# Other costs in the scheduler of a transformer trunk's kernel, and its mLSTM output gate as a product of pairs

## The chip, the cores and the metric

One core of a Trainium2 chip. The time is the device time of one execution in microseconds (us), the median of three runs. Engines: PE is TensorE (matrix products), DVE VectorE, ACT ScalarE, POOL GpSimd; SP issues most of the DMAs.

## The reference

Two decoder layers on 256 tokens of width 1024, all in float32: first an mLSTM layer, then a differential-attention layer with a shared K and V. Each layer adds four sub-layers to x, each between two RMS norms: a half-step FFN, the mixer, a second half-step FFN and a per-layer input embedding. What the change touches is the end of the mLSTM mixer:

```
proj = x @ w_in
q, k, v, o, gates = jnp.split(proj, ...)
...
h = mlstm_chunkwise(q, k, v, log_i, log_f)
h = rms_norm(h, head_norm[:, None, :])
...
return (jax.nn.sigmoid(o) * h) @ w_out
def swiglu(x, w_in, w_out):
    gate, up = jnp.split(x @ w_in, 2, axis=-1)
    return (jax.nn.silu(gate) * up) @ w_out
```

The output gate o is a 256 x 1024 by 1024 x 1024 product, as v is.

## The kernel before

The tokens are two tiles t of 128 rows. A float32 product is made of three fp32r products per 128-row slice of the contraction: high half by high half, low half of the weight by high half of x, high half of the weight by low half of x (`mm3`). Weights come as 1 MB tiles 128x2048 from HBM into eight raw buffers (`wraw`); ACT copies the high half (`whi`), DVE subtracts it for the low half (`wlo`), into six pairs of buffers. In the traces the bank of a product's sum is `accI` (three banks; products by input weights) or `accO` (by output weights, and the heads' numerators), `tr` is the bank of transposes.

`in_block` gives one tile's 512 columns of a product: 8 slices by 3 matmuls, 24. `block_pair` gives both tiles by 1024 columns at once as a 2x2 block product in the manner of Strassen and Winograd: seven products (`times`, 12 matmuls each) where eight would do it plainly. For that it needs sums of weight blocks: `t3` and `u1` are sums made by DMA (a plain load by SP, then an accumulating load on the same buffer by POOL), `wt2` and `wt4` sums made by DVE on top; sums of x blocks (`forms`: s1, s2, s3, n4), and sums of the products (DVE, with the first operand copied out of its bank by ACT, `held`). Before the change block_pair serves the pairs of FFN blocks and the mLSTM's v; the output gate is four `in_block`s (`gate(t, b)`), each followed by a sigmoid on ACT.

In the mixer `outputs(t)` turns the heads' numerators into `hns[t]`: it sums denominators on PE (the 128x1 matmuls), works on 128x4 tiles on DVE, takes a power on POOL (`mhalf`), normalises, and scales the numerators with four DVE operations. `gated(t, b)` multiplies a half of `hns[t]` by the sigmoid and transposes it for the output projection (`out_proj`). Then comes the norm after the sub-layer: squares on ACT, two operations 128x1 on POOL, scaling on DVE, and the transposes for the next sub-layer.

The order is not written out by hand. A first pass records all operations (`Notes`); `play` then simulates a list scheduler with a cost for each operation (`cost`: `dur` is how long it occupies its engine, `lat` when its result is there) and picks, engine by engine, what comes next, and which buffer a tile gets. A second pass issues the operations in that order (all from one line, L389, so the profile's groups tell them apart by tile). DMAs get a landing time from their size; accumulating ones are on a queue of their own. Each engine runs its own queue in order; buffers and data are guarded by semaphores.

## Time and profile before

| | |
|---|---|
| runs | 1012.2, 1009.74, 1011.77 us; median 1011.77 |
| profiled execution | 1012.75 us, of which the span of the trace is 1011.0 |
| busy in the span | PE 99%, weight loads 81%, DVE 84%, ACT 67%, POOL 8% |
| moved by DMA | 262.11 MB, 259 GB/s in the mean |
| granted clock, mean | 0.998 |

The profile's page begins with the busy time of each engine, then shows the span in 40 slices (each digit the busy share in tenths), the chain of work that ended last, and groups of instructions. In a timeline a row has start, length, engine, operation, output and inputs, shapes and count, and in brackets how long the engine was idle before it and what released it.

### The profile page before, as it was taken

To read this page: it belongs to the slowest core of one execution; us is meant where nothing else is said; L and a number is where in the kernel's file an instruction comes from. 1 tells how busy PE (TensorE), PEld (TensorE's weight loads), DVE (VectorE), ACT (ScalarE), POOL (GpSimd) and SP (SyncE) were. 2 spreads that over 40 slices of the span, in tenths; PEclk is the share of its full clock that TensorE was granted. 3 is DMA by queue.
4 is the path that set the end of the run, shared out by engine and by line. 5 is a ranking of instruction groups with operands and counts; after the bars stand their busy time and mean duration, and the time that the engine had idled before them with its cause. 6 is when DMAs were issued, how large, how long until landed. Compare 5 with 4: busy or idle time off the path is not lost.

```text
span 1011.0 us, 12465 instructions
## 1 busy us (share of the span) xinstructions
PE 996.6 (99%) x4692; PEld 815.2 (81%) x4692; DVE 847.1 (84%) x886; ACT 674.3 (67%) x909; POOL 77.3 (8%) x118
## 2 busy tenths in 40 slices
PE   9999999999999999999999999999999999999997
PEld 7887787888878888888887888778778888888786
DVE  6999895888879899987888898986985899999783
ACT  7666683667657767656875677766866767768372
POOL 0000000100121000001110000000101200000010
PEclk9999999999999999999999999999999999999999
DMA  9999974955699788765779998784556997897631
GB/s 341 395 308 296 306 279 152 279 206 198 247 318 277 251 290 263 282 257 172 292 259 327 321 300 301 240 322 170 201 217 235 311 263 235 293 303 269 229 124 43
DMA packets 44132, 262.11 MB, mean 259 GB/s; under 512 B 5288, under 2 KB 5672, under 8 KB 15912
## 3 DMA queue, kind: packets, MB, share of 16 engines
q1 hardware_dynamic: 39176, 227.50, 58.7%
q0 software_dynamic: 4608, 33.56, 17.1%
q8 instruction: 37, 0.61, 0.2%
q10 hardware_dynamic: 288, 0.27, 0.1%
q14 instruction: 23, 0.19, 0.1%
HBM read 250.82 MB, written 10.49 MB: 258 GB/s over the span
## 4 chain that ended last, share of the span: by engine, by line
PE 83%; DMA 7%; DVE 6%; issue 2%; ACT 1%; POOL 0%; SPq 0%; DVEq 0%; POOLq 0%; ACTq 0%
PE accI L389 51%; PE accO L389 28%; DMA wraw<-in_ffn_in 5%; PE tr L389 4%; DVE wraw L389 1%; DVE wlo_4r L389 1%; DMA wraw<-in_x 1%; DVE wlo_3r L389 1%; DMA wraw<-in_xT 1%; DMA att<-in_diff_lambda 1%; DVE wlo_2r L389 1%; DVE wlo_1r L389 1%; DVE att L389 1%; DVE wlo_5r L389 0%; DVE sm L389 0%
## 5 line engine op out<-in xcount | busy, mean ns | idle before, releaser
L389 ACT ACTIVATE whi_0r<-wraw 128x2048 fp32r<-128x2048 f32 (+2 forms) x51 | 74.9, 1477 | 17.1 <-PE accI L389 4.9
L389 ACT ACTIVATE whi_1r<-wraw 128x2048 fp32r<-128x2048 f32 (+2 forms) x52 | 74.7, 1449 | 9.5 <-DMA wraw<-in_ffn_in 3.8
L389 ACT ACTIVATE whi_5r<-wraw 128x2048 fp32r<-128x2048 f32 (+1 forms) x49 | 72.6, 1493 | 9.5 <-DMA wraw<-in_ffn_in 2.5
L389 ACT ACTIVATE whi_2r<-wraw 128x2048 fp32r<-128x2048 f32 (+1 forms) x45 | 70.2, 1571 | 9.3 <-DMA wraw<-in_ffn_in 5.8
L389 ACT ACTIVATE whi_3r<-wraw 128x2048 fp32r<-128x2048 f32 (+1 forms) x47 | 72.2, 1546 | 5.4 <-PE accI L389 2.6
L389 ACT ACTIVATE whi_4r<-wraw 128x2048 fp32r<-128x2048 f32 (+1 forms) x44 | 69.8, 1599 | 8.5 <-DMA wraw<-in_ffn_in 3.4
L389 DVE TENSOR_TENSOR wraw<-wraw,wraw 128x2048 f32<-128x2048 f32 x32 | 73.0, 2282 | 0.1
L389 ACT ACTIVATE att<-accI 128x512 f32<-128x512 f32 x64 | 38.1, 596 | 27.1 <-PE accI L389 26.7
L389 POOL DMA_DIRECT2D wraw<-in_ffn_in x30 | 26.8, 893 | 370.6 <-DMA wraw<-in_ffn_in 287.2
L389 ACT ACTIVATE sg<-accI,sm 128x256 f32<-128x256 f32 x43 | 20.2, 470 | 41.4 <-PE accI L389 30.7
L389 DVE TENSOR_TENSOR wlo_4r<-wraw,whi_5r 128x2048 fp32r<-128x2048 f32 (+1 forms) x25 | 44.0, 1770 | 1.8 <-ACT whi_5r L389 1.8
L389 DVE TENSOR_TENSOR wlo_1r<-wraw,whi_0r 128x2048 fp32r<-128x2048 f32 (+1 forms) x25 | 43.9, 1771 | 1.5 <-ACT whi_0r L389 1.5
L389 DVE TENSOR_TENSOR wlo_5r<-wraw,whi_1r 128x2048 fp32r<-128x2048 f32 (+1 forms) x24 | 44.0, 1839 | 0.1
L389 POOL TENSOR_SCALAR sm<-sm 128x1 f32<-128x1 f32 x32 | 18.6, 582 | 327.3 <-ACT waste L389 327.2
L389 DVE TENSOR_TENSOR wlo_0r<-wraw,whi_0r 128x2048 fp32r<-128x2048 f32 (+2 forms) x24 | 41.8, 1751 | 2.0 <-ACT whi_0r L389 2.0
L389 DVE TENSOR_TENSOR wlo_2r<-wraw,whi_3r 128x2048 fp32r<-128x2048 f32 (+1 forms) x23 | 41.6, 1819 | 1.8 <-ACT whi_3r L389 1.8
L389 DVE TENSOR_TENSOR wlo_1r<-wraw,whi_1r 128x2048 fp32r<-128x2048 f32 (+2 forms) x26 | 42.0, 1626 | 1.1 <-ACT whi_1r L389 1.0
L389 DVE TENSOR_TENSOR wlo_3r<-wraw,whi_4r 128x2048 fp32r<-128x2048 f32 (+1 forms) x22 | 41.5, 1895 | 1.5 <-ACT whi_4r L389 1.5
L389 DVE TENSOR_TENSOR wlo_2r<-wraw,whi_2r 128x2048 fp32r<-128x2048 f32 (+1 forms) x22 | 41.5, 1896 | 1.0 <-ACT whi_2r L389 0.9
L389 DVE TENSOR_TENSOR wlo_4r<-wraw,whi_4r 128x2048 fp32r<-128x2048 f32 (+1 forms) x22 | 41.4, 1896 | 0.7 <-ACT whi_4r L389 0.7
L389 DVE TENSOR_TENSOR wlo_3r<-wraw,whi_3r 128x2048 fp32r<-128x2048 f32 (+1 forms) x22 | 41.5, 1895 | 0.4 <-ACT whi_3r L389 0.4
L389 DVE TENSOR_TENSOR wlo_0r<-wraw,whi_2r 128x2048 fp32r<-128x2048 f32 (+1 forms) x23 | 41.5, 1818 | 0.0
(488 smaller groups left out, 3033.7 us busy)
## 6 DMA issues: line engine op xcount, KB each, us to landing
wraw<-in_ffn_in SPq DMA_DIRECT2D x99, 1024.0 KB, 7.8
wraw<-in_ffn_out SPq DMA_DIRECT2D x44, 1024.0 KB, 10.2
wraw<-in_ffn_in POOLq DMA_DIRECT2D x30, 1024.0 KB, 11.8
wraw<-in_mlstm_in SPq DMA_DIRECT2D x13, 1024.0 KB, 4.8
wraw<-in_ple_gate SPq DMA_DIRECT2D x8, 1024.0 KB, 5.3
wraw<-in_w_kv SPq DMA_DIRECT2D x8, 1024.0 KB, 4.8
home<-wraw SPq DMA_DIRECT2D x28, 256.0 KB, 4.0
wraw<-home SPq DMA_DIRECT2D x14, 512.0 KB, 3.3
```

The lines of the kernel that those rows point to most:

```text
L389: getattr(getattr(self.nc, eng), name)(*args, **kw)
```

## The change

The change has five parts. The scheduler's costs: ACT and DVE operations occupy their engine 100 and 85 ns less, and their results come 100 and 85 ns after that (before 40 and 50); ACT sums and float32 matmuls cost otherwise; an operation that uses a result of its own engine, other than PE, waits for the result and not only for the engine. DMA: the bytes of plain and of accumulating transfers share the transfer engines one third to two thirds while both have some, and the landing times of all that are under way are worked out again with each new issue. In `block_pair` the load of b11 stands first and that of u1 behind b21. The output gate goes through `block_pair`, with `opened` called as each block is there. At the start, eight matmuls on zeros stand where twelve did.

```diff
@@ -214,27 +214,32 @@
         if o.name == "dma_start":
             size = math.prod(c for s, c in outs[0].ap) * 4
             o.dur = {"sync": 450, "scalar": 450, "gpsimd": 900}[o.eng]
-            o.lat = size / (165.0 if o.kw.get("accum_op") is not None else 400.0)
+            o.lat = size / (200.0 if o.kw.get("accum_op") is not None else 390.0)
         elif o.eng == "tensor":
             if o.name == "transpose":
                 o.dur, o.lat = 109, 310
             elif ins[0].dtype == F32R:
                 o.dur, o.lat = n / 2.4 + 14, n / 2.4 + 215
             else:
-                o.dur = max(n * 4 / 2.4 + 6, 70)
+
+                o.dur = max(n * 4 / 2.4 / (2 if ins[0].ap[0][1] == 64 else 1) + 6, 70 if n * 4 < P else 105)
+                if n == 1:
+                    o.dur = 210
                 o.lat = o.dur + 270
         elif o.eng == "scalar":
             ptr = any(k in o.kw and isinstance(o.kw[k], bass.AP) for k in ("scale", "bias"))
-            o.dur = 0.83 * m + (200 if sb_in else 172) + (90 if ptr else 0)
-            o.lat = o.dur + (110 if o.kw.get("accum_out") is not None else 0) + 40
+
+            sums = o.kw.get("accum_out") is not None
+            o.dur = 0.83 * m + (100 if sb_in else 72) + (90 if ptr else 0) + (90 if sums else 0)
+            o.lat = o.dur + (110 if sums else 0) + 140
             f = o.args[2] if len(o.args) > 2 else None
             o.table = f if f in (AF.Silu, AF.Exp, AF.Ln, AF.Sigmoid) else None
         elif o.eng == "vector":
             one = o.name in ("tensor_copy", "tensor_scalar", "memset") and len(sb_in) == len(ins)
-            o.dur = m / 0.96 / (2 if one else 1) + 155 + (60 if o.name == "scalar_tensor_tensor" else 0)
+            o.dur = m / 0.96 / (2 if one else 1) + 70 + (60 if o.name == "scalar_tensor_tensor" else 0)
             if o.name == "tensor_tensor_scan":
-                o.dur = 680
-            o.lat = o.dur + 50
+                o.dur = 600
+            o.lat = o.dur + 135
             o.two = len(sb_in) > 1
         elif o.eng == "gpsimd":
             o.dur = 560 if o.name == "tensor_tensor" else 320 + m
...
@@ -287,8 +294,35 @@
         for o in ops:
             if not o.left:
                 waiting[o.eng].append(o)
-        dma_free = add_free = 0.0
+
+        flow = {False: [], True: []}
+        flow_at = 0.0
         landed = []
+        freed = {}
+
+        def step(queues, t, until, done):
+            while t < until:
+                act = [k for k in queues if queues[k] and queues[k][0][0] <= t]
+                share = {k: 1.0 if len(act) == 1 else (1 / 3, 2 / 3)[k] for k in act}
+                stop = min([until] + [t + queues[k][0][1] / share[k] for k in act]
+                           + [q[0][0] for k, q in queues.items() if q and k not in act])
+                for k in act:
+                    queues[k][0][1] -= (stop - t) * share[k]
+                    if queues[k][0][1] < 1e-6:
+                        done(queues[k].pop(0)[2], stop)
+                t = stop
+                if not any(queues.values()):
+                    break
+
+        def later(q, t):
+            t += 400
+            if t > q.end:
+                q.end = t
+                for u in q.users:
+                    if u.start is None and u.after[q]:
+                        u.ready = max(u.ready, t)
+                for v in freed.get(q, ()):
+                    given[v] = max(given[v], t)
         lock_until = 0.0
         before = "r"
         table = AF.Silu
...
@@ -337,18 +371,15 @@
             waiting[e].remove(o)
             o.start = s
             if o.name == "dma_start":
-                if o.kw.get("accum_op") is None:
-                    begin = max(s + 1900, dma_free)
-                    dma_free = begin + o.lat
-                    o.end = dma_free + 400
-                    if e != "gpsimd":
-                        landed.append(o.end)
-                else:
-
-                    begin = max(s + 4000, add_free)
-                    add_free = begin + o.lat
-                    dma_free = max(dma_free, begin) + o.lat
-                    o.end = add_free + 4000
+                adds = o.kw.get("accum_op") is not None
+                o.end = s
+                if s > flow_at:
+                    step(flow, flow_at, s, lambda q, t: None)
+                    flow_at = s
+                flow[adds].append([s + (2600 if adds else 1700), o.lat, o])
+                step({k: [list(q) for q in v] for k, v in flow.items()}, flow_at, 1e12, later)
+                if e != "gpsimd":
+                    landed.append(o)
                 clock[e] = s + o.dur
             else:
                 end = s + o.dur
@@ -369,7 +400,7 @@
             for u in o.users:
                 u.left -= 1
                 if u.after[o]:
-                    u.ready = max(u.ready, o.end if u.eng != e or o.name == "dma_start" else clock[e])
+                    u.ready = max(u.ready, o.end if u.eng != "tensor" or e != u.eng else clock[e])
                     if u.eng != e:
                         u.far = max(u.far, o.end)
                 else:
...
@@ -503,7 +536,7 @@
     wz = T([P, P], "h", 2)
     nc.vector.memset(wz, 0.0)
     warm = trp()
-    for i in range(12):
+    for i in range(8):
         nc.tensor.matmul(warm[:, :P], wz, wz, start=True, stop=True)
 
 
@@ -673,12 +706,12 @@
             return parts(out)
 
         nc.is_urgent = False
+        b11 = load(src[0])
         t3 = load(src2[0], src2[1])
-        u1 = load(src[0], src2[0])
-        b11 = load(src[0])
         w11 = parts(b11)
         b21 = load(src[1])
         w21 = parts(b21)
+        u1 = load(src[0], src2[0])
         wt2 = add(b11, b11, t3)
         wu1 = parts(u1)
         wt3 = parts(t3)
@@ -1030,15 +1063,6 @@
             hns.append(hn)
 
 
-        wg_ = [in_weights(a["mlstm_in"][4 + b], m=2) for b in range(2)]
-        sos = {}
-
-        def gate(t, b):
-            pi = acc_in()
-            in_block(pi, xts[t], wg_[b])
-            sos[t, b] = piece()
-            nc.scalar.activation(sos[t, b], pi, AF.Sigmoid, scale=rs[t])
-
         uts = [None, None]
 
         def gated(t, b):
@@ -1048,15 +1072,23 @@
             nc.vector.tensor_tensor(hns[t][:, c], hns[t][:, c], sos[t, b], op=ALU.mult)
             to_xt4(hns[t], 4 * b, uts[t])
 
-        gate(0, 0)
-        outputs(0)
-        gated(0, 0)
-        gate(0, 1)
-        gated(0, 1)
-        outputs(1)
-        for b in range(2):
-            gate(1, b)
-            gated(1, b)
+        sos = {}
+
+        def opened(b, t, src):
+            sos[t, b] = piece()
+            nc.scalar.activation(sos[t, b], src, AF.Sigmoid, scale=rs[t])
+            if (t, b) == (0, 0):
+                outputs(0)
+                gated(0, 0)
+            elif (t, b) == (1, 1):
+                outputs(1)
+            elif (t, b) == (0, 1):
+                gated(0, 1)
+            else:
+                gated(1, 0)
+                gated(1, 1)
+
+        block_pair(xts, xf, a["mlstm_in"][4], a["mlstm_in"][5], opened)
         return out_proj(uts, a["mlstm_out"], gbc, epilogue)
```

How the order changes, at four places. The names are those of buffers and what went into them; a number behind a name is the buffer's.

DVE in the gate stretch, before: from the end of v's last split to `hns[0]`. `sm4` are the small tiles of `outputs(0)`; the four SCALAR_TENSOR_TENSOR write `hns[0]`; `att_4` in the last row is a sigmoid.

```order
L389 TENSOR_TENSOR wlo_4r_75<-wraw_3_80,whi_4r_69 128x2048
L389 TENSOR_TENSOR att_7_112<-accI_2_99,att_7_112 128x512
L389 TENSOR_TENSOR wlo_5r_76<-wraw_4_81,whi_5r_70 128x1024 x2
L389 TENSOR_TENSOR wlo_1r_72<-wraw_6_83,whi_1r_66 128x1024 x2
L389 TENSOR_TENSOR wlo_0r_71<-wraw_2_79,whi_0r_65 128x1024 x2
L389 TENSOR_TENSOR wlo_2r_73<-wraw_7_84,whi_2r_67 128x1024 x2
L389 TENSOR_TENSOR sm4_13_143<-sm4_12_142,sm4_11_141 128x4
L389 TENSOR_SCALAR sm4_14_144<-sm4_13_143 128x4
L389 TENSOR_TENSOR sm4_16_146<-sm4_10_140,sm4_15_145 128x4
L389 SCALAR_TENSOR_TENSOR wraw_3_80<-accO_2_102,sm4_16_146,wraw_0_77 128x256 x2
L389 SCALAR_TENSOR_TENSOR wraw_3_80<-accO_3_103,sm4_16_146,wraw_0_77 128x256 x2
L389 TENSOR_TENSOR wraw_3_80<-wraw_3_80,att_4_109 128x512
```

The same stretch in the new order, in two pieces. First the sums and splits at its head (`wlo_5` is b11, `wlo_1` b21, `wlo_3` t3, `accO` and `h` belong to the last heads):

```order
L422 TENSOR_TENSOR wlo_5r_76<-wraw_7_84,whi_5r_70 128x2048
L422 TENSOR_TENSOR att_7_112<-accI_2_99,att_7_112 128x512
L422 TENSOR_TENSOR wraw_7_84<-wraw_7_84,wraw_1_78 128x2048
L422 SCALAR_TENSOR_TENSOR att_4_109<-accO_3_103,at_0_127,h_1_114 128x256
L422 SCALAR_TENSOR_TENSOR att_4_109<-accO_3_103,at_0_127,h_1_114 128x128
L422 TENSOR_TENSOR wlo_1r_72<-wraw_3_80,whi_1r_66 128x2048
L422 SCALAR_TENSOR_TENSOR att_2_107<-accO_0_100,att_4_109 128x384
L422 TENSOR_TENSOR wlo_3r_74<-wraw_1_78,whi_3r_68 128x2048
```

And from the split of wt2 (`wlo_0`) through `hns[0]` to that of wt4 (`wlo_5`); `wraw_3` there is the sum wt4:

```order
L422 TENSOR_TENSOR wlo_0r_71<-wraw_7_84,whi_0r_65 128x2048
L422 TENSOR_TENSOR sm4_13_143<-sm4_12_142,sm4_11_141 128x4
L422 TENSOR_SCALAR sm4_14_144<-sm4_13_143 128x4
L422 TENSOR_TENSOR wraw_3_80<-wraw_3_80,wraw_7_84 128x2048
L422 TENSOR_TENSOR sm4_16_146<-sm4_10_140,sm4_15_145 128x4
L422 SCALAR_TENSOR_TENSOR wraw_1_78<-accO_2_102,sm4_16_146,wraw_0_77 128x256 x2
L422 SCALAR_TENSOR_TENSOR wraw_1_78<-accO_1_101,sm4_16_146,wraw_0_77 128x256 x2
L422 TENSOR_TENSOR wraw_1_78<-wraw_1_78,att_7_112 128x512
L422 TENSOR_TENSOR wlo_2r_73<-wraw_2_79,whi_2r_67 128x2048
L422 TENSOR_TENSOR xl_2r_95<-tr_0_104,xh_2r_91 128x512
L422 TENSOR_TENSOR wlo_4r_75<-wraw_6_83,whi_4r_69 128x2048
L422 TENSOR_TENSOR wlo_5r_76<-wraw_3_80,whi_5r_70 128x2048
```

An addition of 128x2048 stands ahead of b21's split, and another between the operation that POOL waits for and the one that waits for POOL; the four gate splits that were behind each other are now spread, and seven.

POOL at the end of the mLSTM mixer, before. `sm4_15` and `sm4_2` are the powers of `outputs`, the 128x1 pairs the norms after the projection:

```order
L389 TENSOR_TENSOR sm4_15_145<-sm4_14_144,mhalf_0_129 128x4
L389 TENSOR_TENSOR sm4_2_132<-sm4_1_131,mhalf_0_129 128x4
L389 DMA wraw_3_80<-in_ffn_in 128x2048
L389 DMA wraw_4_81<-in_ffn_in 128x2048
L389 TENSOR_SCALAR sm1_1_169<-sm4_4_134 128x1
L389 TENSOR_TENSOR sm1_3_171<-sm1_1_169,mhalf_0_129 128x1
L389 TENSOR_SCALAR sm1_2_170<-sm4_5_135 128x1
L389 TENSOR_TENSOR sm1_5_173<-sm1_2_170,mhalf_0_129 128x1
```

And in the new order:

```order
L422 DMA wraw_5_82<-in_mlstm_in 128x2048
L422 DMA wraw_1_78<-in_mlstm_in 128x2048
L422 DMA wraw_2_79<-in_mlstm_in 128x2048
L422 TENSOR_TENSOR sm4_15_145<-sm4_14_144,mhalf_0_129 128x4
L422 TENSOR_TENSOR sm4_2_132<-sm4_1_131,mhalf_0_129 128x4
L422 TENSOR_SCALAR sm1_1_169<-sm4_4_134 128x1
L422 TENSOR_TENSOR sm1_3_171<-sm1_1_169,mhalf_0_129 128x1
L422 TENSOR_SCALAR sm1_2_170<-sm4_5_135 128x1
L422 TENSOR_TENSOR sm1_5_173<-sm1_2_170,mhalf_0_129 128x1
L422 DMA wraw_3_80<-in_ffn_in 128x2048
```

The two accumulating loads of the next FFN's weights stood ahead of both norms; now the first stands behind them and the second further on. Three accumulating loads of the gate and v stand ahead of the powers.

DVE in the first FFN where PE waited for `hl_2` at 120.96 us, before:

```order
L389 SCALAR_TENSOR_TENSOR h_0_113<-att_0_105,sm1_4_172,sg_1_122 128x256
L389 TENSOR_TENSOR wlo_4r_75<-wraw_0_77,whi_4r_69 128x2048
L389 TENSOR_TENSOR wraw_0_77<-wraw_0_77,wraw_4_81 128x2048
L389 TENSOR_TENSOR hl_2r_120<-tr_0_104,hh_2r_117 128x256
L389 TENSOR_TENSOR wlo_5r_76<-wraw_6_83,whi_5r_70 128x2048
```

And in the new order:

```order
L422 SCALAR_TENSOR_TENSOR h_0_113<-att_0_105,sm1_4_172,sg_1_122 128x256
L422 TENSOR_TENSOR wlo_5r_76<-wraw_5_82,whi_5r_70 128x2048
L422 TENSOR_TENSOR wraw_4_81<-wraw_4_81,wraw_0_77 128x2048
L422 TENSOR_TENSOR hl_2r_120<-tr_0_104,hh_2r_117 128x256
L422 TENSOR_TENSOR wraw_5_82<-wraw_5_82,wraw_4_81 128x2048
```

The sum of weights (`wraw` from two `wraw`) still stands directly ahead of `hl_2`.

SP around the load of lambda (`in_diff_lambda`), near 662 us, before:

```order
L389 DMA wraw_3_80<-in_ffn_out 128x2048
L389 DMA wraw_2_79<-in_ffn_out 128x2048
L389 DMA att_7_112<-in_diff_lambda 128x256
L389 DMA wraw_6_83<-in_ffn_out 128x2048
L389 DMA wraw_5_82<-in_diff_q 128x2048
```

And in the new order:

```order
L422 DMA wraw_7_84<-in_ffn_out 128x2048
L422 DMA wraw_0_77<-in_diff_q 128x2048
L422 DMA wraw_3_80<-in_diff_q 128x2048
L422 DMA att_2_107<-in_diff_lambda 128x256
L422 DMA wraw_4_81<-in_diff_q 128x2048
```

It stood between loads of `ffn_out` and stands behind two of `diff_q`. Where DVE comes to it (the first 128x64 row), in the new order:

```order
L422 TENSOR_TENSOR wlo_2r_73<-wraw_3_80,whi_3r_68 128x1024
L422 TENSOR_TENSOR att_1_106<-att_1_106,att_2_107 128x512
L422 TENSOR_TENSOR wlo_2r_73<-wraw_3_80,whi_3r_68 128x1024
L422 SCALAR_TENSOR_TENSOR h_1_114<-att_1_106,sm1_1_169,sg_0_121 128x256
L422 TENSOR_TENSOR att_4_109<-accI_2_99,att_4_109 128x512
L422 TENSOR_TENSOR wlo_3r_74<-wraw_4_81,whi_4r_69 128x1024 x2
L422 TENSOR_TENSOR wlo_4r_75<-wraw_6_83,whi_5r_70 128x2048
L422 TENSOR_TENSOR att_1_106<-att_2_107 128x64
L422 TENSOR_TENSOR hl_2r_120<-tr_0_104,hh_2r_117 128x256
```

The second `diff_q` load goes to `wraw_3`, which the second row with `wlo_2` frees; four rows of DVE work lie between that and the 128x64 row.

8 lines of the change are left out of this document (6 added, 2 removed).

## The prediction

> **What bounds the kernel now.** I read the head of the profile's page first, then the 40 slices, the chain that ended last, what TensorE (PE) waits for, and windows around the edited places.
>
> ```profile
> span 1011.0 us, 12465 instructions
> PE 996.6 (99%) x4692; PEld 815.2 (81%) x4692; DVE 847.1 (84%) x886; ACT 674.3 (67%) x909; POOL 77.3 (8%) x118
> PE   9999999999999999999999999999999999999997
> DMA  9999974955699788765779998784556997897631
> PE 83%; DMA 7%; DVE 6%; issue 2%; ACT 1%; POOL 0%; SPq 0%; DVEq 0%; POOLq 0%; ACTq 0%
> 353.14 15.67 PE accI L389 x69
> ```
>
> PE is busy 99% of the span and carries 83% of the chain; the last row is an undisturbed stretch of it, 69 matmuls in 15.67 us or 227 ns each. So time goes in two ways: fewer matmuls, or less of what PE still waits for. That second part is small, and the view of PE's waits (us in total, times, longest) lists it whole:
>
> ```profile
> PE tr L389 <- DVE h L389: 2.5, 3, 1.3
> PE tr L389 <- DVE hl_2r L389: 1.2, 1, 1.2
> PE accO L389 <- ACT att L389: 1.1, 2, 0.7
> PE tr L389 <- DVE wraw L389: 1.0, 1, 1.0
> PE accO L389 <- DVE wlo_3r L389: 0.4, 1, 0.4
> PE accI L389 <- DVE h L389: 0.4, 1, 0.4
> PE accI L389 <- ACT att L389: 0.2, 1, 0.2
> ```
>
> They add up to 6.8 us. That bounds what a better order alone can return; span less PE's busy time, 14.4 us, also holds the ends of the program and gaps too short to be listed.
>
> The sum is made against the profiled execution, 1012.75 us: the span of 1011.0 and 1.75 around it. The median of the runs is 1011.77, so 0.98 is taken off at the end. A measurement of this kernel tells about 0.3% from no change, 3.0 us: below 1008.7 counts as faster, above 1014.8 as slower.
>
> **Seven products for eight.** The output gate was four blocks of 24 matmuls; it becomes seven products of 12. Twelve matmuls go: 12 x 227 ns = 2.72 us off PE. The price is elsewhere:
>
> ```profile
> 118.28 2.29 DVE L389 TENSOR_TENSOR wraw<-wraw,wraw 128x2048 f32<-128x2048 f32 x1
> 229.49 1.90 ACT L389 ACTIVATE whi_4r<-wraw 128x2048 fp32r<-128x2048 f32 x1
> 231.29 0.57 ACT L389 ACTIVATE att<-accI 128x512 f32<-128x512 f32 x1
> 241.00 0.69 DVE L389 TENSOR_TENSOR att<-accI,att 128x512 f32<-128x512 f32 x1
> 241.61 2.35 DVE L389 TENSOR_TENSOR wlo_5r<-wraw,whi_5r 128x1024 fp32r<-128x1024 f32 x2
> 215.00:235.00 20.00, 20.00 (x100) 15.80 (x98) 16.93 (x35) 16.23 (x23) 0.00 (x0) 1.00 0.43 158
> 235.00:256.00 21.00, 21.00 (x97) 17.25 (x96) 17.95 (x27) 16.44 (x26) 1.02 (x1) 1.00 0.78 292
> 256.00:276.00 20.00, 20.00 (x105) 16.82 (x104) 16.65 (x28) 12.68 (x22) 1.93 (x1) 1.00 0.58 218
> 276.00:290.00 14.00, 12.99 (x61) 10.50 (x59) 7.14 (x9) 3.50 (x8) 2.68 (x4) 1.00 1.00 336
> ```
>
> (The last four are windows: length, then PE, weight loads, DVE, ACT, POOL busy, clock, DMA share, GB/s.) Seven weight matrices are split instead of four: three more subtractions on VectorE (DVE) at about 2.3 us. Two sums of weights (2.29 each) and three sums of products (0.69) join them: 6.9 + 4.6 + 2.1 = 13.6 us. ScalarE (ACT) gets three splits at 1.90 and about four copies at 0.57, 8.0 us, and has 11.9 idle in 235 to 276. DVE there has only 41 - 34.6 = 6.4 idle, and 6.9 more in 276 to 290. It fits if work can slide into that third window, not otherwise. DMA carries one more plain megabyte and two accumulating ones; at 0.58 to 0.78 of its share I cost that at nothing. The cover is those windows' spare third; with it gone, they push what follows by about 3 MB / 336 GB/s = 9 us of transfers, some of which the eight raw buffers hide.
>
> Whether PE feels DVE's extra work I worked out by walking the new order of DVE, ACT and PE with the durations above. Four places come out late. Between the low halves of b11 and b21 DVE now does 0.69, an addition of 2.29, 0.7 for the last head and the split itself, 2.28: 5.96 us. PE has 24 products meanwhile, 5.45, and three short ones: about 0.3 late. The chain from token tile 0's heads to the transposes of `hns[0]` is the largest:
>
> ```profile
> 253.46 0.16 DVE L389 TENSOR_TENSOR sm<-sm,sm 128x4 f32<-128x4 f32 x1 [1.14 <-POOL sm L389]
> 253.66 1.66 DVE L389 SCALAR_TENSOR_TENSOR wraw<-accO,sm,wraw 128x256 f32<-128x256 f32 x4
> ```
>
> Where DVE idled 1.14 for POOL, the new order has a 2.29 addition: the chain is 1.15 later, and I take 1.1 as wait on the transposes. Behind that transpose PE's whole queue waits: t3's product, b22's, and the start of the output projection. The first low half of `mlstm_out` (0.25) and the transposes after the projection (0.45) are the others. New waits: +2.1 us. From both sides: 0, if DVE's start into the stretch is early enough (it idles 3.1 us in 215 to 235), and 7.2 us, if only the 6.4 idle of the first two windows can be used (13.6 - 6.4). I take 2.1, being nearest to the walk's rows, and keep both ends.
>
> **The new order, named places.** One place is removed for a reason that order and trace show together, at the end of the mixer's projection:
>
> ```profile
> 286.64 0.86 POOL L389 DMA_DIRECT2D wraw<-in_ffn_in  x1 [2.23 <-ACT waste L389]
> 287.59 0.30 POOL L389 TENSOR_SCALAR sm<-sm 128x1 f32<-128x1 f32 x1
> 288.00 0.39 PE L389 MATMUL accO<-whi_4r,xl_1r 128*128 128x512 f32 x1
> 288.58 1.42 DVE L389 SCALAR_TENSOR_TENSOR wraw<-wraw,sm,wraw 128x512 f32<-128x512 f32 x2 [2.72 <-POOL sm L389]
> 289.39 0.66 PE L389 MATMUL tr<-ident,wraw 128*128 128x128 f32 x4 [1.00 <-DVE wraw L389]
> ```
>
> POOL issues an accumulating DMA for 0.86 us just ahead of the norm's two scalar steps; DVE and then PE wait behind it: PE's matmul before the transposes starts at 288.00, the transposes 1.39 later, 1.16 over the pitch of 0.227. In the new order they stand behind both tiles' norms: -1.15. For DMAs that now come later I charge nothing: their weights belong to the next FFN, whose first plain loads stand ahead of them; uncovered, the first would arrive 2 x (0.30 + 0.57) later. POOL's three issues ahead of the powers cost nothing while they come early: it idles 12.76 us before the second power, and more before the first; one held up there by a raw buffer would delay `hns[0]` by as much.
>
> ```profile
> 266.18 1.93 POOL L389 TENSOR_TENSOR sm<-sm,mhalf 128x4 f32<-128x4 f32 x1 [12.76 <-DVE sm L389]
> ```
>
> Other named waits are 6.8 - 1.0 = 5.8. I keep three:
>
> ```profile
> 120.96 0.44 PE L389 MATMUL tr<-ident,h 128*128 128x128 f32 x2 [1.17 <-DVE hl_2r L389]
> 50.00:120.00 70.00, 69.61 (x311) 56.63 (x309) 62.88 (x49) 46.31 (x46) 3.85 (x5) 1.00 0.98 307
> 546.47 1.92 ACT L389 ACTIVATE whi_2r<-wraw 128x2048 fp32r<-128x2048 f32 x1 [3.85 <-DMA wraw<-in_ffn_in]
> 549.39 0.44 PE L389 MATMUL tr<-ident,h 128*128 128x128 f32 x2 [1.27 <-DVE h L389]
> att<-in_diff_lambda SPq DMA_DIRECT2D x1, 128.0 KB, 6.2
> 668.48 0.22 DVE L389 TENSOR_TENSOR att<-att 128x64 f32<-128x64 f32 x1 [1.76 <-DMA att<-in_diff_lambda]
> ```
>
> The one at 120.96 stays: the same additions and subtractions stand ahead of `hl_2`, in a stretch where DMA is 98% busy. So do the 0.4 behind lambda (its load now waits behind two `diff_q` loads for a buffer, and DVE reaches it some 5.8 us of work after that buffer is free, against 6.2 to land) and the 0.4 in the first 25 us, which the arrival of weights sets. Of the other 3.8 I take half, -1.9. Nothing reorders away a late transfer as at 546.47, though b11 ahead of the accumulated t3 in every pair gives PE something to do sooner. Ends: -3.8, and +1.5 if waits of the same kind appear elsewhere; I took the middle of the listed amount, being unable to see more.
>
> **The start.** Eight warm-up matmuls replace twelve.
>
> ```profile
> 1.04 5.49 PE L389 MATMUL tr<-h 128*128 128x128 f32 x24 [1.04 <-DVE h L389]
> 6.18 1.19 PE L389 MATMUL accI<-whi_0r,xh_0r 128*128 128x512 f32 x2
> 8.14 0.62 PE L389 MATMUL accI<-whi_0r,xh_0r 128*128 128x512 f32 x2
> 20.97 0.50 PE L389 MATMUL accI<-whi_2r,xh_0r 128*128 128x512 f32 x1 [0.40 <-DVE h L389]
> ```
>
> Twelve leave 24 records at about 213 ns, so eight save 8 x 0.213 = 1.7 us at most; the first product then starts near 5 instead of 6.18. But DMA is the limit up to 120 us, and what PE gains there it waits for later: 0, with ends -0.7 and +1.5. The upper end is from the rows: a pair at 6.18 takes 1.19, one at 8.14 0.62, so matmuls run at half rate until about 7.2; if that moved 3 us later, some 7 matmuls cost 0.2 more each. The Trainium skill, "TensorE: Matmul & The Clock Gate", Part 1, speaks against this edit: full clock comes after a sustained busy window of about 3.4 us, and the window runs freely. By that rule eight (16 x 0.213 = 3.4 us, estimate) may fail to fill one; then the sum would be about 1.5 higher. The change to full rate at 7.2 us, 6.2 after the first matmul, agrees with no more than two windows.
>
> **Sum.** 1012.75 - 2.72 + 2.1 - 1.15 - 1.9 + 0 = 1009.08 in a profiled execution; less 0.98, 1008.1 by the median.
>
> **Rivals.**
> (1) The order does better: of the 5.8 nearly all but the one at 120.96 (4.6) goes, and the gate adds only 1.0 of waits. 1011.77 - 2.72 + 1.0 - 1.15 - 4.6 = 1004.3. For it: the waits are short, single places; against: three of them end in a late DMA.
> (2) The saving is not seen: DVE's extra work costs PE the whole 2.72, and of the others only the 1.15 at 288 goes: 1011.77 - 1.15 = 1010.6, up to 1011.8 if new short waits replace it. For it: PE already runs at 99%, so the new costs have nothing but the last per cent to work on; DVE is 84% busy. This is also the case in which the change does not do what it says.
> (3) Slower: DVE becomes the bound of the gate stretch. With only 6.4 us of the 13.6 absorbed, PE waits 7.2 and saves 2.72: 1011.77 + 4.5 = 1016.3. It is slower by more than 3.0 as soon as DVE absorbs less than 13.6 - 5.7 = 7.9. Against it: 6.9 more idle behind, and the accumulators let PE run ahead of the sums.
> (4) The clock at the start: my sum plus 1.5, 1009.6; it decides nothing but faster against same.
>
> **How the numbers follow.** Forecast, 1006.5 to 1009.5: 0.40, of which 0.28 lies below 1008.7. Rival 1: 0.25. Rival 2: 0.20. Rival 4: 0.07. Rival 3: 0.08. Faster by over 0.3%: 0.28 + 0.25 = 0.53; same: 0.12 + 0.20 + 0.07 = 0.39; slower: 0.08. The range leaves out rival 3 and the outer part of rival 1: from 1003.3 to 1013.0, the upper end being rival 2 with the 1.5 of the start on top.
>
> **What would show it.** Right: twelve fewer products of 512 columns on PE; no wait near the end of the mixer's projection; a wait of about 1 us on the transposes of `hns[0]`; DVE over 90% busy from the gate to the projection's middle; the wait on `hl_2` still there at about 120. Wrong: PE waiting on `wlo` or on `xl` several times between b11 and b22 (rival 3), the first products at double pitch beyond 8 us (rival 4), or new waits at FFN starts where loads were reordered.

## The result, and the profile after

| kernel | runs | median us | range us | ratio, 95% interval |
|---|---|---|---|---|
| before | 4 | 1010.75 | 1008.73 to 1012.2 | |
| changed | 4 | 1027.53 | 1023.45 to 1028.91 | 1.0161 (1.0125 to 1.0197) |

The changed kernel is slower by 16.8 us. The forecast was 1008.1, which is 2.7 below these four runs of the kernel before, and the result lies outside the range. Its profiled execution took 1026.71 us, of which 1024.9 are the span. The head of its page, the counts of accumulating loads, and what PE waited for:

```profile
span 1024.9 us, 12474 instructions
PE 1000.7 (98%) x4672; PEld 815.4 (80%) x4672; DVE 855.7 (83%) x890; ACT 679.9 (66%) x912; POOL 85.3 (8%) x120
wraw<-in_ffn_in POOLq DMA_DIRECT2D x30, 1024.0 KB, 12.5
PE tr L422 <- DVE hl_0r L422: 5.4, 2, 3.4
PE tr L422 <- DVE hl_2r L422: 4.2, 2, 2.2
PE tr L422 <- DVE h L422: 1.6, 2, 1.0
PE accI L422 <- DVE wlo_1r L422: 1.4, 1, 1.4
PE tr L422 <- DVE wraw L422: 1.3, 1, 1.3
PE tr L422 <- DVE hl_1r L422: 1.3, 1, 1.3
PE accO L422 <- DVE wlo_0r L422: 0.6, 1, 0.6
```

PE has twenty instructions fewer (twelve products, and four matmuls for warming up, which stand as eight records) and is busy 4 us longer: some of its matmuls ran at half rate. Its listed waits were 6.8 us; the rows here make 15.8. The view of waits says where: most are the transposes of h in the FFNs (`hl_0`, `hl_1`, `hl_2`, `h`), 11.4 us in six places. (The seventh place in these rows is the 1.04 us before PE's first warm-up matmul, which the kernel before has too.) The windows of before (first) and of the changed kernel (second), in FFN stretches (the last three numbers are the granted clock, DMA share and GB/s):

```profile
300.00:450.00 150.00, 150.00 (x680) 122.22 (x679) 137.06 (x117) 102.14 (x108) 7.96 (x10) 1.00 0.83 277
850.00:900.00 50.00, 50.00 (x225) 40.55 (x225) 47.65 (x34) 34.32 (x32) 2.62 (x3) 1.00 0.85 271
```

```profile
300.00:450.00 150.00, 146.74 (x655) 118.61 (x654) 138.12 (x117) 100.92 (x106) 8.92 (x11) 0.99 0.88 296
850.00:900.00 50.00, 46.62 (x204) 37.72 (x203) 43.91 (x35) 31.93 (x32) 1.76 (x2) 0.97 0.79 251
```

PE gets through 25 matmuls less in the first and 21 less in the second, in stretches that the change was not thought to touch for the worse. The longest wait, in the timeline of the changed kernel, by engines (POOL, ACT, DVE, PE):

```profile
844.70 0.87 POOL L422 DMA_DIRECT2D wraw<-in_ffn_in  x1 [12.64 <-DMA wraw<-in_ffn_in]
858.37 1.92 ACT L422 ACTIVATE whi_1r<-wraw 128x2048 fp32r<-128x2048 f32 x1 [3.95 <-PE accO L422]
860.19 0.45 ACT L422 ACTIVATE sg<-accI,sm 128x256 f32<-128x256 f32 x1
862.35 0.37 ACT L422 ACTIVATE hh_0r<-tr 128x256 fp32r<-128x256 f32 x1
860.68 0.48 DVE L422 SCALAR_TENSOR_TENSOR h<-accI,sm,sg 128x256 f32<-128x256 f32 x1 [3.53 <-ACT sg L422]
863.28 0.42 DVE L422 TENSOR_TENSOR hl_0r<-tr,hh_0r 128x256 fp32r<-128x256 f32 x1
859.99 0.39 PE L422 MATMUL accO<-whi_2r,hh_1r 128*128 128x512 f32 x1
863.75 0.69 PE L422 MATMUL tr<-ident,h 128*128 128x128 f32 x2 [3.38 <-DVE hl_0r L422]
864.67 1.05 PE L422 MATMUL accO<-wlo_0r,hh_1r 128*128 128x512 f32 x2
866.79 0.39 PE L422 MATMUL accI<-wlo_2r,xh_2r 128*128 128x512 f32 x1
```

The reading: POOL issues an accumulating load at 844.70; it lands 13.6 us later, at 858.3 (from the landing records of the trace). ACT's next instruction is that weight's high half, so ACT stands idle for 3.95 us. (The releaser named is `accO`, but PE's last product with the old content of that buffer had started at 852.7; the start coincides with the landing.) Behind it in ACT's queue wait `sg`, which DVE needs for h, and `hh_0`, which DVE needs for `hl_0`; the next transposes need the bank that `hl_0` frees. PE stands from 860.4 to 863.75, and the two matmuls from 864.67 take 0.42 us each where 0.227 is the pitch: half rate until 866.8. Three of the other long waits look alike: whi_2 on ACT at 352.47, whi_5 at 384.38 and whi_3 at 584.57 each start when an accumulating load lands (issued 339.2, 371.5 and 572.2; 13.2, 12.8 and 12.3 us under way). The sixth place, 2.23 us at 679.91, is another: there DVE waits for the load of lambda, a plain one.

That points to the planner's formula. By the old one an accumulating megabyte is there 4.0 + 1048576 / 165 + 4.0 = 14.4 us after its issue at the earliest; the loads take 11.8 us in the median (page of before). By the new one, if no other accumulating load is ahead of it, it is there after 2.6 + 1048576 / 200 + 0.4 = 8.2 us, or 10.9 when it shares all along with plain loads; they take 12.5 in the median. In the median the old plan was 2 to 3 us on the safe side, and the new one is early. A plan that believes a weight to be there puts its split at the head of ACT's queue, and all behind it waits.

### The profile page after: what moved, and what is told of

The parts are those of the page before. It is cut to its first block, busy times and chain, and to the rows that moved or that the text cites. A ratio compares the mean times of both kernels' runs of the same rounds, so it can differ in the third digit from the quotient of the medians.

```text
span 1024.9 us, 12474 instructions
## 1 busy us (share of the span) xinstructions
PE 1000.7 (98%) x4672; PEld 815.4 (80%) x4672; DVE 855.7 (83%) x890; ACT 679.9 (66%) x912; POOL 85.3 (8%) x120
## 5 line engine op out<-in xcount | busy, mean ns | idle before, releaser
L422 DVE TENSOR_TENSOR wraw<-wraw,wraw 128x2048 f32<-128x2048 f32 x34 | 77.6, 2283 | 4.4 <-DMA wraw<-in_mlstm_in 2.2
L422 ACT ACTIVATE whi_2r<-wraw 128x2048 fp32r<-128x2048 f32 (+1 forms) x49 | 74.0, 1526 | 9.6 <-DMA wraw<-in_ffn_in 5.5
L422 ACT ACTIVATE whi_4r<-wraw 128x2048 fp32r<-128x2048 f32 (+1 forms) x48 | 74.2, 1556 | 7.7 <-PE accI L422 5.7
L422 ACT ACTIVATE whi_5r<-wraw 128x2048 fp32r<-128x2048 f32 (+1 forms) x43 | 69.8, 1633 | 9.7 <-DMA wraw<-in_ffn_in 3.0
L422 ACT ACTIVATE att<-accI 128x512 f32<-128x512 f32 x68 | 40.6, 597 | 23.9 <-PE accI L422 23.7
L422 POOL TENSOR_SCALAR sm<-sm 128x1 f32<-128x1 f32 x32 | 22.4, 699 | 326.0 <-ACT waste L422 326.0
L422 PE MATMUL tr<-ident,h 128*128 128x128 f32 x176 | 35.4, 283 | 11.5 <-DVE hl_0r L422 5.4
L422 DVE TENSOR_TENSOR wlo_2r<-wraw,whi_3r 128x2048 fp32r<-128x2048 f32 (+1 forms) x24 | 44.0, 1839 | 2.2 <-ACT whi_3r L422 2.1
L422 PEld LDWEIGHTS tr<-ident,h 128*128 128x128 f32 x176 | 22.0, 141 | 28.9 <-DVE hl_0r L422 9.0
L422 DVE TENSOR_TENSOR wlo_3r<-wraw,whi_4r 128x2048 fp32r<-128x2048 f32 (+1 forms) x25 | 44.0, 1772 | 0.5 <-ACT whi_4r L422 0.4
## 6 DMA issues: line engine op xcount, KB each, us to landing
wraw<-in_ffn_in POOLq DMA_DIRECT2D x30, 1024.0 KB, 12.5
```

Source lines behind the costliest of these rows:

```text
L422: getattr(getattr(self.nc, eng), name)(*args, **kw)
```

## The experiments

Theory D: the loss is the new landing estimate of accumulating loads, by this chain. Rival C: the shorter ScalarE and VectorE costs pack the queues too tightly. Rival G: the gate pair is the loss. Rival N: any other order loses, since the old one is a picked one. Every ratio below is against runs of the kernel before on the same chip; a ratio whose interval holds 1 shows no difference.

### The landing estimate

e1_sums_late, the changed kernel with one number other:

```diff
         def later(q, t):
-            t += 400
+            t += 400 if q.kw.get("accum_op") is None else 4000
```

> The changed kernel with one number changed: the planner takes an accumulating load to be there 4000 ns after its bytes have flowed, as the old planner did, and not 400. Theory D (the new landing estimate of accumulating loads, 10.9 us at most by its formula against 12.5 measured, puts weights at the head of ScalarE's queue before they are there): the four long PE waits of the FFNs (1.4 + 2.1 + 2.1 + 3.5) and the half-rate matmuls behind them (about 4.5) go, so 1027.5 - 13.7 = about 1014, range 1010 to 1018. Theory C (the shorter ScalarE and VectorE costs pack the queues too tightly): the waits stay, over 1022.

1017.60 against 1011.66, ratio 1.0067 (1.0048 to 1.0087), where the changed kernel has 1.0161: 9.9 us better. The window from 300 to 450 us and that from 850 to 900:

```profile
300.00:450.00 150.00, 149.68 (x677) 121.40 (x676) 142.19 (x122) 106.17 (x114) 12.10 (x12) 1.00 0.91 306
850.00:900.00 50.00, 50.00 (x228) 40.90 (x228) 49.18 (x39) 37.40 (x36) 2.62 (x3) 1.00 0.92 300
```

The four FFN waits behind accumulating loads are gone, as D expects and C does not. The time is inside D's range and 3.6 above its middle value. The plan still has the wait behind lambda (1.93 at 679.84), and another at the head of the mLSTM:

```profile
219.91 1.47 PE L422 MATMUL accO<-wraw 128*128 128x256 f32 x8
223.34 0.50 PE L422 MATMUL accI<-whi_1r,xh_0r 128*128 128x512 f32 x1 [1.96 <-ACT xh_0r L422]
224.86 0.79 PE L422 MATMUL accI<-whi_0r,xh_0r 128*128 128x512 f32 x1 [0.64 <-ACT xh_0r L422]
229.35 0.63 PE L422 MATMUL accI<-wlo_1r,xh_0r 128*128 128x512 f32 x1
237.54 0.40 PE L422 MATMUL accI<-wlo_0r,xh_0r 128*128 128x512 f32 x1
```

Two short stops, and PE then runs at half rate until 237.4.

e11_old_dma_model, the changed kernel with all of the old DMA model:

```diff
-            o.lat = size / (200.0 if o.kw.get("accum_op") is not None else 390.0)
+            o.lat = size / (165.0 if o.kw.get("accum_op") is not None else 400.0)
...
-                flow[adds].append([s + (2600 if adds else 1700), o.lat, o])
-                step({k: [list(q) for q in v] for k, v in flow.items()}, flow_at, 1e12, later)
+                    begin = max(s + 4000, add_free)
+                    add_free = begin + o.lat
+                    dma_free = max(dma_free, begin) + o.lat
+                    o.end = add_free + 4000
```

> The changed kernel with the whole old DMA model in its planner; costs, gate, load order and eight warm-up matmuls as changed. Theory D: no wait over 1.5 us in the FFNs behind an accumulating load; what is left is the gate's price and chance places, 1013 to 1019. If the loss is the costs' or the load order's: 1022 or more.

1011.33 against 1011.02, ratio 1.0012 (0.9995 to 1.0029), better than D's range. The costs, the gate pair, the load order and the eight warm-up matmuls together cost nothing that can be told; the DMA model on top of them costs the 15 us. In these FFN stretches PE is as busy as before:

```profile
300.00:450.00 150.00, 149.59 (x679) 122.08 (x677) 138.87 (x119) 103.37 (x112) 11.87 (x11) 1.00 0.89 298
850.00:900.00 50.00, 50.00 (x227) 40.93 (x226) 49.58 (x37) 39.53 (x36) 3.51 (x4) 1.00 0.90 299
```

One clause of D's expectation failed: a wait of 1.95 us on the transposes of h is left at 545.37, and behind it DVE had idled 2.45 us for an accumulating load (issued 529.17, 13.4 us under way). The old estimate makes such places rare, not impossible.

e10_sums_early goes the other way, from the kernel before:

```diff
-                    begin = max(s + 4000, add_free)
+                    begin = max(s + 2600, add_free)
...
-                    o.end = add_free + 4000
+                    o.end = add_free + 400
```

> The kernel before with two numbers of its planner changed: an accumulating load begins after 2600 ns (was 4000) and is there 400 ns after its bytes (was 4000), so 9.4 us at the least where 11.5 to 12.5 are measured. Nothing else of the change. Theory D: waits of 1 to 5 us on the FFNs' transposes behind accumulating loads, 1015 to 1022. If the early estimate harms only together with the rest: 1009 to 1013.

1016.53 against 1011.02, ratio 1.0051 (1.0034 to 1.0069), inside D's range. One long wait is new (POOL, ACT, PE):

```profile
560.03 0.88 POOL L389 DMA_DIRECT2D wraw<-in_ffn_in  x1 [1.46 <-DVE wraw L389]
578.86 1.91 ACT L389 ACTIVATE whi_1r<-wraw 128x2048 fp32r<-128x2048 f32 x1 [6.29 <-DMA wraw<-in_ffn_in]
584.67 0.44 PE L389 MATMUL tr<-ident,h 128*128 128x128 f32 x2 [4.44 <-DVE hl_2r L389]
```

The load came second on POOL's queue and was under way 18.7 us, and the one ahead of it had been issued 2.35 us before. By the old numbers it is there 4.0 + 2 x 6.36 + 4.0 - 2.35 = 18.4 us after its issue, by the early ones 13.4.

e2_dma_only, the kernel before with the whole new DMA model (e11's diff the other way round):

> The kernel before with only the planner's new DMA model (sharing, new latencies); costs, gate, load order and warm-up as before. Theory D: most of the loss is there, 1018 to 1026, with PE waits of 1 to 4 us behind accumulating loads in the FFNs. Theory C: within 4 us of before, 1007 to 1015.

1019.39 against 1011.66, ratio 1.0084 (1.0059 to 1.0108), inside D's range. Here too a weight at the head of ACT's queue is late, and PE's next transposes start 4.8 us late:

```profile
540.21 1.91 ACT L417 ACTIVATE whi_2r<-wraw 128x2048 fp32r<-128x2048 f32 x1 [9.83 <-DMA wraw<-in_ffn_in]
```

But by its semaphore this split waits for a plain load, issued by SP at 526.29 and 13.9 us under way; the two accumulating loads near it land at 538.1 and 544.9. Another loss, 1.8 us at 477.5, is behind a plain load of ple_gate. So the time is as D says and the mechanism is of its shape, but neither of the two long waits is behind an accumulating load: the DMA model as a whole puts late weights at the head of ACT's queue, and D as worded names only part of it.

### The other parts by themselves

e3_costs_only, the kernel before with the changed lines of `cost` for PE, ACT and DVE and the rule on an engine's own results:

```diff
-            o.dur = 0.83 * m + (200 if sb_in else 172) + (90 if ptr else 0)
+            o.dur = 0.83 * m + (100 if sb_in else 72) + (90 if ptr else 0) + (90 if sums else 0)
...
-            o.lat = o.dur + 50
+            o.lat = o.dur + 135
...
-                    u.ready = max(u.ready, o.end if u.eng != e or o.name == "dma_start" else clock[e])
+                    u.ready = max(u.ready, o.end if u.eng != "tensor" or e != u.eng else clock[e])
```

> The kernel before with only the new costs of ScalarE, VectorE and float32 matmuls and the rule that an operation waits for a result of its own engine; DMA model, gate, load order and warm-up as before. Theory D: 1006 to 1013, no PE wait over 1.5 us in the FFNs behind an accumulating load. Theory C: 1018 or more.

1014.10 against 1011.66, ratio 1.003 (1.001 to 1.005), 1.1 above D's range and 3.9 below C's. Its longest wait of PE is 2.2 us, at 632.4; behind it ACT had idled 3.17 for a plain load. As the whole of the loss, C falls.

e4_gate_only, the kernel before with the hunk of the gate alone:

```diff
-        gate(0, 0)
...
+        block_pair(xts, xf, a["mlstm_in"][4], a["mlstm_in"][5], opened)
```

> The kernel before with only the output gate as a pair of seven products. If the gate's price is what the prediction said (2.7 saved, 2.1 of new waits): 1009 to 1012 beside a before of about 1011. If the changed kernel's 4 us more of lost PE time between 200 and 300 us belong to the gate pair as such: 1012 to 1015. If the gate pair were the cause of the whole loss: over 1020.

1022.57 against 1011.66, ratio 1.0119 (1.0096 to 1.0142): on the old planner the pair loses 10.9 us. That is the value named for the pair as the cause of the whole loss; e5 below and e11 above speak against it. PE's longest wait there, with what follows it:

```profile
277.02 0.80 PE L389 MATMUL accI<-wlo_5r,xh_3r 128*128 128x512 f32 x1 [4.61 <-DVE wlo_5r L389]
277.61 0.63 PE L389 MATMUL accI<-whi_5r,xl_3r 128*128 128x512 f32 x1
```

`wlo_5` is wt4's split. It stands on DVE behind the whole chain of the second tile's heads; splits count as less urgent than the chain in the scheduler.

e9_gate_wt4_urgent makes that sum and split urgent:

```diff
+        nc.is_urgent = urgent
         wt4 = add(b21, b21, b11)
```

> The run with the pair alone on the old planner, with one thing changed: the sum and the split of wt4 in the gate are recorded as urgent, so that VectorE does not put the second tile's heads ahead of them. Theory V (the pair's price is the place of wt4's split on VectorE's queue): the wait of 4.8 us on its low half and the half-rate matmuls behind it (about 2.2) go, 1022.6 - 7 = about 1015.5, range 1012 to 1018. If the wait only moves to the transposes of the second tile's heads: over 1019.

1022.14 against 1011.02, ratio 1.0116 (1.0101 to 1.0131): no gain. The wait is now at the transposes of the heads (1.49 on `wraw`, then 0.69 on `xh_0`), and a place near 409 us, where ACT waits for a plain load of an FFN weight, costs 2.4 instead of 1.8. The price of the pair is not the place of one split.

e5_old_gate, the changed kernel with the four blocks of the old gate:

> The changed kernel with the four blocks of the old output gate; all else (planner, load order, eight warm-up matmuls) as changed. PE's lost time between 200 and 300 us was 7.7 us with the pair and 3.7 before; if that comes back and 2.7 of matmuls are added, about 1026, range 1022 to 1030. If the pair itself costs what the run with the pair alone cost (10.9 us), 1014 to 1019.

1020.43 against 1012.05, ratio 1.0088 (1.0057 to 1.0119): between the two expectations. It still has a wait of 4.4 us behind an accumulating load (whi_3 on ACT at 855.58 after 4.98 idle). G is not the whole loss: without the pair half of it is still there.

e12_old_dma_old_gate, the same with the old DMA model, so e11 without the pair:

> The run with the old DMA model (all else as changed) with the old gate put back: new costs, new load order, eight warm-up matmuls. If the pair loses time under a sound planner (the run with the pair lost 9.7 us of PE time between 200 and 300 us, before 3.7): 1011.3 + 2.7 - 6.0 = about 1008, range 1006 to 1010. If the pair pays its twelve matmuls there: 1012 to 1015.

1013.24 against 1012.19, ratio 1.0006 (0.9987 to 1.0025), where e11 has 1.0012. With the old DMA model and the new costs no gain or loss of the pair can be told. That its waits eat its twelve matmuls, about as the prediction's 2.72 and 2.1 said, fits this, but the intervals are near 2 us either way.

e15_load_order_only, the kernel before with the new order of loads in `block_pair`:

```diff
+        b11 = load(src[0])
         t3 = load(src2[0], src2[1])
-        u1 = load(src[0], src2[0])
-        b11 = load(src[0])
...
+        u1 = load(src[0], src2[0])
```

> The kernel before with only the new order of loads in block_pair (b11 first, u1 behind b21). Theory D says nothing of it but that the accumulating loads are issued a little later: 1009 to 1014. If the load order alone brings the waits behind accumulating loads: over 1016.

1021.26 against 1012.19, ratio 1.0094 (1.0078 to 1.0111): over 1016, so the load order alone brings such waits, which theory D did not say. The chain of ACT, DVE and PE is the one of D:

```profile
606.36 0.86 POOL L389 DMA_DIRECT2D wraw<-in_ffn_in  x1 [12.74 <-DMA wraw<-in_ffn_in]
619.73 1.92 ACT L389 ACTIVATE whi_3r<-wraw 128x2048 fp32r<-128x2048 f32 x1 [3.85 <-DMA wraw<-in_ffn_in]
624.23 0.44 PE L389 MATMUL tr<-ident,h 128*128 128x128 f32 x2 [2.33 <-DVE hl_2r L389]
```

But this load took 13.4 us and the old estimate is 14.4 at least: here it isn't the estimate of the landing that was early. POOL had itself waited 12.74 us for the plain load of the same buffer, so the issue may have been later than planned; that was not tried. With the new costs the same load order is harmless (e12). So with the old DMA model a plan can lose nearly 1% too, and the early estimate is not the only way to a late weight.

### Smaller parts

e6_warm12, the changed kernel with `range(12)` for the warm-up:

> The changed kernel with twelve warm-up matmuls. In the changed kernel PE ran at half rate until 9.9 us, before until 7.2. If that is the warm-up's doing, full rate comes by about 7 us again and the first 50 us lose 1.1 us less: 1025 to 1027, a difference at the edge of what can be told; the rows of the start tell it better. If the window at the start is a matter of chance, the rows look as in the changed kernel.

1023.97 against 1012.05, ratio 1.0127 (1.0088 to 1.0166), below the range expected; the interval overlaps that of the changed kernel. The start of the changed kernel and of this one:

```profile
1.04 3.79 PE L422 MATMUL tr<-h 128*128 128x128 f32 x16 [1.04 <-DVE h L422]
8.57 0.63 PE L422 MATMUL accI<-wlo_0r,xh_0r 128*128 128x512 f32 x1
10.39 0.39 PE L422 MATMUL accI<-whi_0r,xh_0r 128*128 128x512 f32 x1
```

```profile
1.04 4.81 PE L422 MATMUL tr<-h 128*128 128x128 f32 x24 [1.04 <-DVE h L422]
5.60 0.71 PE L422 MATMUL accI<-whi_0r,xh_0r 128*128 128x512 f32 x2
8.16 0.39 PE L422 MATMUL accI<-whi_0r,xh_0r 128*128 128x512 f32 x1
```

With eight, the products take 0.43 us each until 9.9 us; with twelve they begin at full rate at 5.60. Before, also with twelve, full rate came at 7.2, so where it falls varies. Over all runs: of the five traces with eight, the changed kernel and e12 stay at half rate until about 10 us, while e1, e5 and e11 are at full rate by 6.8; the twelve traces with twelve are there by 7.5. So the prediction's rival 4 happened in the changed kernel, at about 1 us, but eight matmuls do not always bring it.

e7_margin330, the kernel before with `MARGIN = 330`:

> The kernel before with one number of the planner changed that belongs to no part of the change (its margin of 300 ns set to 330), so another order as good by the planner's own costs. Theory N (the order before was a picked one, and any other order loses several us to chance waits): 1014 to 1020. Otherwise within 3 us of before.

1011.06 against 1012.05, ratio 1.0 (0.9975 to 1.0025), inside 3 us of before. It says little on N, since the order hardly moved: POOL's and SP's are the same, and PE, DVE and ACT differ in 14, 19 and 8 places.

e8_late_old_gate, the changed kernel with e1's number, the old gate, twelve warm-up matmuls, and the load of lambda recorded ahead:

> The changed kernel with accumulating loads landing 4000 ns later in the plan, the old gate, twelve warm-up matmuls and the load of lambda recorded ahead of the queries. Theory D with the gate's cost: the long waits at the FFNs, in the gate and behind lambda all go; what is left of the change is sharing, costs and load order, 1008 to 1014. If the remaining loss is of another kind (theory N), 1014 or more.

1018.92 against 1012.05, ratio 1.0076 (1.0054 to 1.0097), above D's range and where N was put. It has e1's wait at the mLSTM's head again (2.0 and 0.8 on `xh_0`, half rate behind it), which e11 does not have to that size: mending one number of the new DMA model is not the old model. Recorded earlier, lambda's load was still issued at 665.38, and DVE waited 2.14 for it.

e13_old_dma_lambda, e11 with twelve warm-up matmuls and 5000 ns more for lambda's landing in the plan:

```diff
-                    o.end = dma_free + 400
+                    o.end = dma_free + (5400 if "lambda" in o.args[1].tensor.name else 400)
```

> The run with the old DMA model, with twelve warm-up matmuls, and the planner told that the load of lambda lands 5000 ns later than its bytes say; it moves the products of lambda on VectorE behind three of the FFN's splits of h. The wait of 1.8 us behind lambda goes, and PE is at full rate 2 to 3 us sooner at the start: 1.8 + about 1 less, 1008.5, range 1006.5 to 1010.5. If lambda's wait is only passed on: 1010 to 1012.

1014.13 against 1012.19, ratio 1.0015 (0.9999 to 1.0031). Both values expected were missed. The lambda operations stand behind two `hl` splits at 676.03 and wait for nothing, but the time is not better: a wait of 0.6 at 194.6 came in, and PE spent two short stretches at half rate, near 229 and 266.

e14_best, old DMA model, old gate, twelve, lambda's landing told, new costs and load order:

> Old DMA model, old gate, twelve warm-up matmuls, lambda's landing told, with the new costs and the new load order. If both of the readings above hold: 1003 to 1008, faster than before and than the changed kernel. If the new costs lose what the run with them alone lost (2.4): 1010 to 1014.

1010.83 against 1012.19, ratio 0.999 (0.9975 to 1.0005): not to be told from before, and not the 1003 to 1008 hoped for. No kernel here beats the one before by more than its interval.

## Why the prediction was wrong

**The step that failed** is "Other named waits": -1.9, with ends -3.8 and +1.5 "if waits of the same kind appear elsewhere". They appeared elsewhere: of PE's full list in the changed kernel, 16.8 us, 3.3 are in the gate, so 13.5 stand against the 5.8 of this term, +7.7 where -1.9 was said. About 6 us more went into slow products of 512 columns, most of them at half rate, the start's among them; the sum had no term for these but the start's. The prediction read the new DMA model only as a cause of moved rows, and never set its numbers against the landing times on the page: 11.8 us for the loads from POOL, 8.2 to 10.9 in the formula. e11 shows the DMA model to be the cause: with the old one nothing is lost. e1 shows the landing of accumulating loads to be the larger part: with that one number the four long FFN waits go, and 9.9 of the 16 us.

Even the list of 5.8 was read too generously: it holds the 1.04 us before PE's first warm-up matmul, which no order can return, so the end at -3.8 and rival 1's 4.6 were out of reach by that much. (The range's upper end, rival 2's 1011.8 and the start's 1.5, comes to 1013.3 and not 1013.0; nothing hangs on it.)

**The half-priced wait.** Every wait was costed at its length. The rows of the changed kernel at 864.67, and of e1 at 229.35, show that a stop of two to four microseconds can be followed by 3 to 14 us at half rate, so a long wait can cost half as much again or more.

**The gate.** The saving of 2.72 held in its count: 3952 products of 512 columns against 3964. Of the four places of new waits three were right: b21's split, the transposes of `hns[0]`, the first low half of `mlstm_out`:

```profile
240.41 2.29 DVE L422 TENSOR_TENSOR wraw<-wraw,wraw 128x2048 f32<-128x2048 f32 x1 [1.92 <-DMA wraw<-in_mlstm_in]
245.61 0.50 PE L422 MATMUL accI<-wlo_1r,xh_2r 128*128 128x512 f32 x1 [1.38 <-DVE wlo_1r L422]
258.74 0.65 PE L422 MATMUL tr<-ident,wraw 128*128 128x128 f32 x4 [1.30 <-DVE wraw L422]
278.27 0.73 PE L422 MATMUL accO<-wlo_0r,xh_2r 128*128 128x512 f32 x2 [0.63 <-DVE wlo_0r L422]
```

The sizes were 1.38, 1.30 and 0.63 where 0.3, 1.1 and 0.25 were said: 3.3 us in all for 2.1, inside the ends. The fourth, 0.45 at the transposes after the projection, did not come. The first was mis-sized because the walk took t3 to be there: DVE waited 1.92 for it, an accumulating load once more. In place of DMA "at nothing", the landing belonged in the walk.

**POOL ahead of the norm.** Right: the wait on `wraw` at the end of the mixer's projection is gone.

**The three that were to stay.** The wait at 120.96 did not stay, none is listed there. Lambda's grew from 0.4 to 2.2: DVE idles 2.40 for it, since the load took 7.6 us where 6.2 was counted; DVE's 5.8 us of work were the right count. The 0.4 of the first 25 us is still a 0.4, at 5.24 in place of 20.97.

**The start** was put at 0 with rival 4 at 0.07; rival 4 happened, about +1.

**The rivals.** Rival 3, the one on the slow side, was put in the gate, on DVE's load. The loss was on the slow side by another mechanism: ACT's queue behind a late weight, in the FFNs, where the profile before showed one such place (whi_2 at 546.47, 3.85 idle) that the prediction quoted and read as a thing that reordering can't mend, instead of one that reordering can multiply.

**Left open.** The parts alone lose 0.84% (DMA model), 0.3% (costs), 1.19% (gate) and 0.94% (load order), which together is twice the whole; without the DMA model they lose nothing together. Which numbers of the DMA model make up the 6 us between e1 and e11 was not tried; the late plain loads of e2 point at its plain side. Why the new costs make the gate and the load order harmless was not tried either. N in its plain form does not hold, since e11 to e14 are four more orders and all lie within 0.15% of before; but of the single changes made to the kernel before every one lost but e7's, so the old order may be a lucky one for the old costs. Another order, as good by the same planner, would be needed to tell.

## What to carry to other kernels

Where a planner's numbers change, set each against the trace's time for the same thing before walking the order: an estimate on the early side puts late data at the head of an in-order queue, and everything behind it is late. What one on the safe side costs, no run here shows. In a kernel whose TensorE is 99% busy, a reordering has one per cent to gain and no such limit on the other side. Change an estimate and a work-saving step one at a time; here their effects don't add.

## What the hardware showed that was not expected

PE fell to half rate after short stops. In the changed kernel, the stop and the first row back at full rate:

```profile
386.51 0.39 PE L422 MATMUL accI<-wlo_2r,xh_1r 128*128 128x512 f32 x1
388.88 0.69 PE L422 MATMUL tr<-ident,h 128*128 128x128 f32 x2 [1.98 <-DVE hl_0r L422]
392.35 0.39 PE L422 MATMUL accI<-whi_3r,xh_1r 128*128 128x512 f32 x1
```

About 2 us without a matmul were enough, and the half rate lasted 3.4 us. But a stop of 2.23 us before the transposes of h at 679.91 was followed by no slow matmul, so length alone doesn't decide it. The granted clock does tell: in each of the 17 traces it changes only at whole multiples of 3.41 us from its first change. Here are four such steps, PE alone (busy time, then granted clock, DMA share, GB/s), the first two around the stop above, the last two around the one at 679.91:

```profile
385.49:388.90 3.41, 1.43 (x8) 1.00 0.46 127
388.90:392.31 3.41, 3.41 (x9) 0.50 0.63 209
675.62:679.03 3.41, 2.06 (x10) 1.00 0.92 288
679.03:682.44 3.41, 2.53 (x12) 1.00 1.01 428
```

The first stop lies inside one step, which is 1.98 us idle, and the next step has half the clock. The second stop is cut by a step's end into 1.35 and 0.88 us, and the clock stays. Over all traces, a step at full clock with 1.8 us or more of idle PE was followed by a step at half clock in 14 cases of 14, one with 0.6 to 0.95 in none of 31, and those between in 5 of 46.

The Trainium skill, "TensorE: Matmul & The Clock Gate", Part 1, puts the fall after at least one idle window of about 3.4 us. The length of the step agrees; but the step at 385.49 held 1.43 us of work, so here it need not be idle throughout.

An accumulating megabyte took 7.9 to 18.7 us from issue to landing in these runs, and 128 KB of lambda 4.7 to 8.1. What sets the time of one load was not tried.
